# Second mixer: two decay projections of a head as seven block products instead of sixteen half-size ones, weight sums made by adding transfers

## The chip, the cores and the metric

The kernel runs on one core of a Trainium2 chip. The metric is device time in microseconds (us) for one execution of the whole program, median of several runs. The engines are TensorE (PE in the profile; its weight loads are PEld), VectorE (DVE), ScalarE (ACT), GpSimd (POOL) and SyncE (SP), which issues most of the transfers. All work in program order, each engine in its own queue; semaphores connect them.

## The reference, cut to what matters

Two layers of a diffusion backbone. The change is in the mixer of the second layer (`_odd_mixer`). `h` is the normed, modulated stream of 768 tokens (512 latent, then 256 context), 1024 wide; `w_in` is 1024 x 5120. Each of 8 heads has 128 query columns and 128 columns of decay logits for each direction:

```python
fq, f_fwd, f_bwd, fi, fog = _split(h @ w_in, ODD_SIZES)
q = _heads(jax.nn.silu(fq), HGRN_HEADS)
i = _heads(fi, HGRN_HEADS)
for d, f in enumerate((f_fwd, f_bwd)):
    log_f = jnp.logaddexp(jnp.log(lb[d]), jnp.log1p(-lb[d]) + jax.nn.log_sigmoid(_heads(f, HGRN_HEADS)))
    k = -jnp.expm1(log_f)
    dirs.append(_directional_scan(q, k, i, log_f, n_ctx, reverse=(d == 1)))
o_lat = _gated_readout(dirs[0][1] + dirs[1][1], og[:, :, n_ctx:], out_norm)
```

With s = sigmoid(f) the decay is `lb + (1-lb) s` and k is `(1-lb) - (1-lb) s`: two affine maps of the sigmoid with one scale and one bias per column. The context part is scanned first and gives the state `S0` from which the latent scan starts.

## The kernel before, in words

Every product of 32-bit operands is made of three matmuls on split operands: X = H + L, where H is X rounded by an ACT cast and L is the rest, by a DVE subtraction; the products are H·H, H·L and L·H (`mm3`). `h` lies on the chip split in this way for the whole mixer (tiles x: four of 128 x 3072). A weight is loaded as `raw` by SP, cast to `wH` by ACT (L803) and subtracted to `wL` by DVE (L804).

`odd_mixer` runs over 8 heads. For head hd a generator `prep` makes the decays of both directions and the query; a second generator, `head` (that is `scan`), does the chunked scan of the head's 512 latent tokens and its readout. In `prep` each direction d loads one unit of 1024 x 128 weights (512 KB) and does 48 matmuls of 128 x 256 (tokens 512 to 767) and 128 x 512 (tokens 0 to 511) each into the tile `ff`: 24 of either kind. ACT takes the sigmoid into `sg` (L1419) and one affine map of it each for the context and the latent tokens (L1424, L1426), DVE the other (L1423, L1425). Then 24 matmuls of 128 x 512 give `fq`, the query.

The order of the work is written out by hand: the loop calls `go(...)` with the steps of three heads in turn (query and decays of head hd, scan of head hd-1, readout of hd-2), and `pinned` keeps matmuls and transposes in that order. The other engines' instructions are placed around it by a scheduler at build time; once placed, an engine's queue is fixed. `raw` has three buffers of 512 KB, `wH` and `wL` four each, so a head's weights are fetched, cast and split well ahead of their matmuls.

In `scan`, DVE and ACT alternate over seven levels: ACT copies half of `arr` into `qkh` (L1012), DVE multiplies it by a decay (L1017) and squares up the decays (L1018). PE makes the score blocks (`pch`, `pbh`), transposes (`knph`, `kcT`), state updates (`pdh`) and the output (`poh`); ACT copies `pbh` to `STh` (L1049) and `knph` to `knh` (L1064), which `pdh` needs. In the readout POOL makes the reciprocal root (`rs`, L686).

The feed-forward of the first layer already multiplies by seven block products (`SEVEN`, `seven`), and its down projection already lets transfers from POOL add to what is on the chip (L1773).

Of the kernel before, what the change touches and what calls it, by code (L numbers as in the profile page):

```python
# [8 lines left out]
F32 = mybir.dt.float32  # L9
# [307 lines left out]
class Net:  # L317
# [24 lines left out]
    def banks(self, narrow):  # L342
        if self.ps is not None:
            self.ps.release()
        self.narrow = narrow
        self.ps = self.tc.alloc_tile_pool(name={True: "psn", False: "psw", None: "pso"}[narrow], bufs=1, space=PSUM, reuse_waits="tile")
# [21 lines left out]
    def sc_tile(self, name, which=None):  # L368
        if which is None:
            self.side = which = 1 - self.side  # L370
        return self.ps.tile([P, 512], F32, tag=f"sc{which}", bufs=1, name=name)

# [574 lines left out]
    def scan(self, pool, nm, arr, q, ksum, dscale, f, nt, hpp, V, first, ends, o_evac):  # L947
# [24 lines left out]
        CT = pool.tile([P, ns, 32], F32, tag="CT", bufs=1 if hpp > 1 else 2, name=f"CT{nm}")  # L972
# [29 lines left out]
        while b < P:  # L1002
            qk = pool.tile([P, 2, N], F32, tag=f"qk{N}", bufs=4 if N > CTX else 3, name=f"qk{nm}{b}")
# [64 lines left out]
        for d, (order, steps) in enumerate(orders):  # L1068
# [10 lines left out]
            for i, t in enumerate(steps):  # L1079
                S = pool.tile([P, P], F32, tag="S", bufs=8 if hpp > 1 else 10, name=f"S{nm}{d}{t}")  # L1080
# [318 lines left out]

    def odd_mixer(self, h, fi):  # L1400
        nc, I = self.nc, self.I
        w = I["odd_w_in"][0]
        with self.pool("hg") as gp:
            ones = gp.tile([P, CTX], F32, tag="ones", name="ones")
            nc.gpsimd.memset(ones, 1.0)
            def prep(hd, given):
# [3 lines left out]
                ks = gp.tile([P, SEQ], F32, tag="ks", bufs=2, name=f"ks{hd}")  # L1410
                S0, kcs = [], []
                for d in range(2):
                    pt = self.mm_tile(f"ff{hd}{d}")
                    W = self.unit_cols(w, (1 + d) * D + hd * P)
                    self.gemm_T(pt, W, h, ((512, 256),))
                    yield
                    self.gemm_T(pt, W, h, ((0, 512),))
                    sg = gp.tile([P, NT], F32, tag="sg", bufs=2, name="sg")
                    nc.scalar.activation(sg, pt[:, :NT], AF.Sigmoid)  # L1419
                    lb, lb1, nlb1 = (x[:, d, hd : hd + 1] for x in (self.lb, self.lb1, self.nlb1))  # L1420
                    fc = gp.tile([P, CTX + 32], F32, tag="fc", bufs=2, name="fc")
                    kc = gp.tile([P, CTX], F32, tag="kc", bufs=2, name="kc")
                    nc.vector.tensor_scalar(fc[:, :CTX], sg[:, SEQ:], lb1, lb, op0=ALU.mult, op1=ALU.add)  # L1423
                    nc.scalar.activation(kc, sg[:, SEQ:], AF.Identity, bias=lb1, scale=nlb1)  # L1424
                    nc.vector.tensor_scalar(f[:, d, :], sg[:, :SEQ], lb1, lb, op0=ALU.mult, op1=ALU.add)  # L1425
                    nc.scalar.activation(arr[:, 2 * d, :], sg[:, :SEQ], AF.Identity, bias=lb1, scale=nlb1)  # L1426

                    pr = gp.tile([P, CTX], F32, tag="pr", bufs=1, name="pr")
                    if d == 0:
                        nc.vector.memset(pr[:, CTX - 1 : CTX], 1.0)  # L1430
                        nc.vector.tensor_tensor_scan(
                            pr[:, 0 : CTX - 1][:, ::-1], fc[:, 1:CTX][:, ::-1], ones[:, 1:CTX], 1.0, op0=ALU.mult, op1=ALU.mult
                        )
                    else:
                        nc.vector.memset(pr[:, 0:1], 1.0)
                        nc.vector.tensor_tensor_scan(
                            pr[:, 1:CTX], fc[:, 0 : CTX - 1], ones[:, 1:CTX], 1.0, op0=ALU.mult, op1=ALU.mult
                        )
                    nc.vector.tensor_tensor(kc, kc, pr, op=ALU.mult)

                    kcs.append(kc)
                    yield
                pq = self.mm_tile(f"fq{hd}")
                self.gemm_T(pq, self.unit_cols(w, hd * P), h, ((0, 512),))
                q = gp.tile([P, SEQ], F32, tag="q", bufs=2, name=f"q{hd}")
                nc.scalar.activation(q, pq[:, :SEQ], AF.Sigmoid)
                nc.vector.tensor_tensor(q, q, pq[:, :SEQ], op=ALU.mult)
                nc.vector.tensor_tensor(arr[:, 1, :], q, f[:, 1, :], op=ALU.mult)
                nc.vector.tensor_tensor(arr[:, 3, :], q, f[:, 0, :], op=ALU.mult)
                nc.vector.tensor_tensor(ks, arr[:, 0, :], arr[:, 2, :], op=ALU.add)  # L1450
                given.append((arr, q, ks, f, S0))
                yield
                kns = []
                for kc in kcs:
                    pk = self.tr_tile("kcT")
                    for i in range(2):
                        self.tr(pk[:, i * P : (i + 1) * P], kc[:, i * P : (i + 1) * P], self.ident)
                    kn = gp.tile([P, CTX], F32, tag="kcn", bufs=2, name="kcn")
                    nc.scalar.copy(kn, pk[:, :CTX])
                    kns.append(kn)  # L1460
# [51 lines left out]
            def go(*xs):  # L1512
                for x in xs:
                    next(x, None)
# [770 lines left out]
```

## Time and profile before

| | |
|---|---|
| median of 3 runs | 1674.99 us (1674.77 to 1675.28) |
| the profiled execution's own time | 1675.78 us |
| its span, first to last instruction | 1674.0 us |
| mean granted clock of TensorE | 0.998 |
| PE busy | 1644.8 us, 98% of the span |
| DVE busy | 1311.1 us, 78% |
| ACT busy | 916.1 us, 55% |
| POOL busy | 129.4 us, 8% |
| the mixer's heads on PE | 982 to 1221 us of the span |

The profiled execution took 1.8 us more than its span, and lies 0.8 us above the median. Rows of a profile name the line, the engine, the operation, what is written and read (`out<-in`), the shape, the count, and then busy time and the mean duration of one in ns. A line of a helper stands for many calls: L355 is every matmul, so groups are told apart by the tile written (`ff`, `fq`, `poh`).

### The profile page before, as it was taken

How to read it: one execution, taken by the hardware profiler on the slowest of the kernel's cores; microseconds unless marked ns; L12 is line 12 of the kernel's file. 1: busy time of each engine (PE TensorE's matmuls, PEld its weight loads, DVE VectorE, ACT ScalarE, POOL GpSimd, SP SyncE). 2: the span in 40 equal slices, each digit the busy share in tenths (PEclk: the TensorE clock that was granted, in tenths of full speed). 3: DMA queues.
4: the chain of work that ended last, by engine and by line, in shares of the span. 5: the costliest groups of instructions: out<-in, count | busy, mean ns of one | idle time of the engine just before them, and what ended most of it. 6: DMA issues, size and time to landing. Idle time of an engine off the chain costs nothing.

```text
span 1674.0 us, 32524 instructions
## 1 busy us (share of the span) xinstructions
PE 1644.8 (98%) x13407; PEld 1481.1 (88%) x13407; DVE 1311.1 (78%) x2097; ACT 916.1 (55%) x1551; POOL 129.4 (8%) x139
## 2 busy tenths in 40 slices
PE   9999999999999999999999999999999999999998
PEld 7899987888999999998887888888888899999886
DVE  5999678976898988777668648788775599987887
ACT  5745567845544443446447436666664565555664
POOL 2004110011000000002102000000000100000310
PEclk9999999999999999999999999999999999999999
DMA  9641012164243445249525541121124333333973
GB/s 336 213 132 41 3 45 86 50 227 160 80 126 114 139 151 176 78 153 205 100 84 193 200 127 57 48 65 40 51 65 150 126 114 115 114 101 102 226 164 138
DMA packets 184736, 204.79 MB, mean 122 GB/s; under 512 B 7142, under 2 KB 141836, under 8 KB 184588
## 3 DMA queue, kind: packets, MB, share of 16 engines
q1 hardware_dynamic: 173996, 181.98, 34.7%
q0 software_dynamic: 9024, 17.30, 5.9%
q10 hardware_dynamic: 1568, 3.43, 0.6%
q8 instruction: 105, 1.72, 0.4%
q14 instruction: 43, 0.35, 0.1%
HBM read 193.23 MB, written 9.46 MB: 121 GB/s over the span
## 4 chain that ended last, share of the span: by engine, by line
PE 83%; DVE 8%; ACT 3%; DMA 3%; issue 2%; POOL 0%; SPq 0%; DVEq 0%; ACTq 0%; POOLq 0%
PE nat L355 12%; PE a L355 10%; PE ff L355 8%; PE E L355 7%; PE oproj L355 6%; PE x L355 6%; PE o L355 5%; PE D L355 4%; PE b L355 3%; PE fq L355 3%; PE gqk L355 2%; PE pearly L355 2%; PE q L355 2%; PE S L355 2%; PE poh L355 1%
## 5 line engine op out<-in xcount | busy, mean ns | idle before, releaser
L355 PE MATMUL nat<-wH,x 128*128 128x256 f32 (+2 forms) x968 | 226.7, 322 | 1.2 <-ACT x L2014 0.6
L860 ACT CAST wH<-raw 128x1024 fp32r<-128x1024 f32 x120 | 124.8, 1051 | 102.7 <-DVE raw L885 40.7
L355 PEld LDWEIGHTS nat<-wH,x 128*128 128x128 f32 x968 | 161.9, 190 | 19.5 <-ACT natq L1196 1.7
L861 DVE TENSOR_TENSOR wL<-raw,wH 128x1024 fp32r<-128x1024 f32 x120 | 145.7, 1222 | 23.6 <-ACT wH L860 23.3
L355 PE MATMUL nat<-wL,x 128*128 128x256 f32 (+2 forms) x484 | 153.5, 317 | 1.8 <-DVE wL L804 1.8
L804 DVE TENSOR_TENSOR wL<-raw,wH 128x1024 fp32r<-128x1024 f32 x79 | 95.8, 1222 | 50.6 <-ACT wH L803 49.8
L355 PE MATMUL ff<-x,wH 128*128 128x512 f32 (+1 forms) x512 | 127.6, 340 | 0.0
L686 POOL TENSOR_TENSOR rs<-ms,neghalf 128x1 f32<-128x1 f32 (+2 forms) x56 | 60.1, 1076 | 777.7 <-DVE ms L684 777.6
L803 ACT CAST wH<-raw 128x1024 fp32r<-128x1024 f32 x79 | 82.2, 1050 | 68.5 <-PE ff L355 19.7
L355 PE MATMUL oproj<-wH,x 128*128 128x512 f32 x320 | 102.2, 394 | 0.4 <-ACT x L1330 0.4
L355 PEld LDWEIGHTS nat<-wL,x 128*128 128x128 f32 x484 | 92.1, 190 | 7.8 <-DVE wL L804 2.7
L615 DVE SCALAR_TENSOR_TENSOR macc<-mraw,scT,macc 128x1024 f32<-128x1024 f32 x70 | 88.0, 1282 | 11.6 <-DMA mraw<-in_mod_w_dram 11.4
L355 PEld LDWEIGHTS ff<-x,wH 128*128 128x128 f32 x512 | 87.3, 190 | 10.0
L355 PE MATMUL x<-wH,two 128*128 128x512 f32 x280 | 90.5, 392 | 0.9 <-DVE y L1851 0.7
L1773 POOL DMA_DIRECT2D t<-in_ffn_w_down_dram x36 | 41.9, 1200 | 640.1 <-DVE t L1812 338.3
L1012 ACT COPY qkh<-arr 128x512 f32<-128x512 f32 x112 | 70.2, 641 | 36.6 <-DVE arr L1017 32.3
L355 PE MATMUL ff<-x,wL 128*128 128x256 f32 (+1 forms) x256 | 86.2, 337 | 0.0
L885 DVE TENSOR_TENSOR raw<-raw 128x512 f32<-128x512 f32 x120 | 82.8, 690 | 2.8
L1017 DVE TENSOR_TENSOR arr<-arr,f 128x512 f32<-128x512 f32 x112 | 74.4, 688 | 2.0 <-ACT qkh L1012 0.3
L355 PEld LDWEIGHTS oproj<-wH,x 128*128 128x128 f32 x320 | 59.9, 188 | 13.0 <-ACT x L1330 1.0
L355 PE MATMUL a<-T,wH 128*128 128x384 f32 (+1 forms) x320 | 70.5, 309 | 0.6 <-ACT qb L923 0.5
L355 PE MATMUL E<-T,wH 128*128 128x384 f32 (+1 forms) x320 | 70.4, 309 | 0.7 <-DVE go L938 0.7
(425 smaller groups left out, 4558.6 us busy)
## 6 DMA issues: line engine op xcount, KB each, us to landing
mraw<-in_mod_w_dram SPq DMA_DIRECT2D x80, 512.0 KB, 4.4
raw<-in_ffn_w_gate_dram SPq DMA_DIRECT2D x44, 512.0 KB, 3.9
raw<-in_ffn_w_up_dram SPq DMA_DIRECT2D x44, 512.0 KB, 4.9
raw<-in_odd_w_in_dram SPq DMA_DIRECT2D x40, 512.0 KB, 3.7
t<-in_ffn_w_down_dram POOLq DMA_DIRECT2D x30, 512.0 KB, 8.3
raw<-in_ffn_w_down_dram SPq DMA_DIRECT2D x28, 512.0 KB, 8.0
mraw<-in_mod_w_dram SPq DMA_DIRECT2D x32, 256.0 KB, 6.3
raw<-in_even_w_in_dram SPq DMA_DIRECT2D x16, 512.0 KB, 5.9
```

What stands on the lines that cost most here:

```text
L355: return self.pin(self.nc.tensor.matmul(*a, **k))
L615: nc.vector.scalar_tensor_tensor(a, u, w, a, op0=ALU.mult, op1=ALU.add)
L686: nc.gpsimd.tensor_tensor(rs, ms, self.neghalf.to_broadcast([P, w]), op=ALU.pow)
L803: self.casts = self.casts[-1:] + [nc.scalar.copy(H[:, :m], raw[:, :m])]
L804: vector.tensor_tensor(L[:, :m], raw[:, :m], H[:, :m].bitcast(F32), op=ALU.subtract)
L860: self.nc.scalar.copy(H, f)
L861: self.nc.vector.tensor_tensor(L, f, H.bitcast(F32), op=ALU.subtract)
L885: add = lambda o, x, y: nc.vector.tensor_tensor(o, x, y, op=ALU.add)
L1012: nc.scalar.copy(qkv[:, :, :, half, :], dst)
L1017: nc.vector.tensor_tensor(dst, dst, tb, op=ALU.mult)
L1773: add = lambda o, src: self.pin(nc.gpsimd.dma_start(out=o, in_=src, accum_op=ALU.add))
```

## The change

For heads 1 to 7 the two directions' projections become one product of a 256 x 1024 by a 1024 x 768 matrix, cut into two by two blocks on each side: the weight's blocks are `11`, `12` (forward columns, upper and lower 512 rows) and `21`, `22` (backward columns); `h`'s blocks are the first and second 512 rows by the first and second 384 tokens. Seven products of 512 x 128 by 512 x 384 (12 matmuls of 128 x 384 each) replace the eight that plain block multiplication needs. They use sums of weight blocks and of `h` blocks. Head 0 is done plainly, with eight products.

- `half_sums` makes the four sums of `h` blocks (T1 to T4) once, by DVE subtractions and additions of 128 x 1536 with splits, stepwise ahead of and between the products of head 0.
- The weight sums of a head: blocks are fetched by SP in six pieces of 256 KB; four transfers from POOL with `accum_op=ALU.add` then add further blocks from DRAM into tiles on the chip. `u2` gets two of them one after the other, `u1` and `w21` one each. A seventh operand is made by a DVE addition (`w12 + u2`).
- Seven operands and the query's two halves are each cast and split as 128 x 512, into a ring of four slots that lies in two of the four `wH`/`wL` buffers; the other two hold the scan's level copies (`levels`), which had buffers of their own (`qkh`).
- The four results are put together by ACT copies and four DVE operations on 128 x 384 (`c11`, `c12`, `c21`, `c22`, halves of two `sg` tiles); then the sigmoids. All four affine maps are ACT's now.
- The context's running product is written over `fc`; the readout's squares are written back to PSUM; a few tiles of the scan have fewer buffers. PSUM has single banks for this mixer (`banks(4)`), also under the gate product at the end, whose first weights go into the T tiles.

```diff
+    def half_sums(self, h, pool, temp):
...
+        def steps():
+            op(a, f32["22"][0], f32["12"][0], ALU.subtract)
+            op(b, f32["22"][1], f32["12"][1], ALU.subtract)
+            op(a, a, b, ALU.add)
+            split("T3", a)
...
+            op(a, a, f32["21"][1], ALU.subtract)
+            yield
+            split("T4", a)
...
+            ring = [[own[x][i // 2][:, 512 * (i % 2) : 512 * (i % 2) + 512] for x in "HL"] for i in range(4)]
+            levels = [own[x][i].rearrange("p (a n) -> p a n", a=2) for i in (2, 3) for x in "HL"]
...
+            order = [SEVEN[i] for i in (0, 4, 3, 1, 6, 2, 5)]
...
+            def raw():
+                r = self.wp.tile([P, WU], F32, tag="raw", bufs=3, name="raw")
+                return [r[:, 512 * i : 512 * i + 512] for i in range(2)]
+            def fetch(o, src):
+                nc.sync.dma_start(out=o.rearrange("p (k n) -> p k n", k=4), in_=src)
+            def add(o, src):
+                self.pin(nc.gpsimd.dma_start(out=o.rearrange("p (k n) -> p k n", k=4), in_=src, accum_op=ALU.add))
+            def operand(x):
+                H, L = turned(ring)
+                nc.scalar.copy(H, x)
+                nc.vector.tensor_tensor(L, x, H.bitcast(F32), op=ALU.subtract)
+                return [z.rearrange("p (k n) -> p k n", k=4) for z in (H, L)]
+            def weights(hd):
+                (w11, w12), (w21, w22) = x = raw(), raw()
...
+                u2, u1 = raw()
+                fetch(u2, block(0, 0, hd))
+                fetch(u1, block(1, 0, hd))
+                add(u2, block(1, 0, hd))
+                add(u1, block(1, 1, hd))
+                add(u2, block(1, 1, hd))
+                add(w21, block(0, 0, hd))
+                for x in (w11, w22, u2, u1, w21, w12):
+                    yield operand(x)
+                nc.vector.tensor_tensor(w12, w12, u2, op=ALU.add)
+                yield operand(w12)
...
-                for d in range(2):
-                    pt = self.mm_tile(f"ff{hd}{d}")
-                    W = self.unit_cols(w, (1 + d) * D + hd * P)
-                    self.gemm_T(pt, W, h, ((512, 256),))
-                    yield
-                    self.gemm_T(pt, W, h, ((0, 512),))
...
-                    nc.vector.tensor_scalar(f[:, d, :], sg[:, :SEQ], lb1, lb, op0=ALU.mult, op1=ALU.add)
+                    for wn, xn, b in order:
...
+                        product(pt, next(W), forms[xn], new, True)
+                        if wn == "11":
+                            nc.scalar.copy(c11, pt)
+                        elif wn == "22":
+                            nc.scalar.mul(c21, pt, -1.0)
+                            yield
...
+                            nc.vector.tensor_tensor(c12, c12, pt, op=ALU.add)
+                            sigmoid(c12)
+                            gates(0)
                     yield
...
-                self.gemm_T(pq, self.unit_cols(w, hd * P), h, ((0, 512),))
+                for k, x in enumerate(raw()):
+                    fetch(x, w[512 * k : 512 * k + 512, hd * P : hd * P + P].rearrange("(k p) m -> p k m", p=P))
+                    H, L = operand(x)
+                    product(pq, (H, L), [h.tiles[k][i][:, :, :SEQ] for i in range(2)], k == 0, k == 1)
...
-                go(scan, new)
-                go(outs, old)
-                go(new, new)
-                go(outs, old, scan)
-                go(new, new)
+                go(scan, old, new)
+                go(outs)
+                go(new)
+                go(old, outs, scan)
+                go(new, new, old)
                 go(scan, scan)
```

Where the instructions stand, at three places. POOL's queue in the mixer before: one `rs` for each head's readout.

```order
L686 TENSOR_TENSOR rs_11392<-ms_11390,neghalf_97 128x4
L686 TENSOR_TENSOR rs_11810<-ms_11808,neghalf_97 128x4
L686 TENSOR_TENSOR rs_12228<-ms_12226,neghalf_97 128x4
L686 TENSOR_TENSOR rs_12646<-ms_12644,neghalf_97 128x4
L686 TENSOR_TENSOR rs_13064<-ms_13062,neghalf_97 128x4
```

POOL's queue now, heads 5 and 6: `raw_12134` is the tile of u2 and u1 of head 5, `raw_12129` that of w21 and w22; `raw_12553` and `raw_12548` are head 6's. The three additions into a u tile are u2, u1, u2.

```order
L1485 DMA raw_12134<-in_odd_w_in_dram 128x4x128 x3
L1485 DMA raw_12129<-in_odd_w_in_dram 128x4x128
L689 TENSOR_TENSOR rs_12250<-ms_12248,neghalf_97 128x4
L1485 DMA raw_12553<-in_odd_w_in_dram 128x4x128 x3
L1485 DMA raw_12548<-in_odd_w_in_dram 128x4x128
L689 TENSOR_TENSOR rs_12669<-ms_12667,neghalf_97 128x4
```

Four transfers now stand in the queue ahead of each `rs`.

ACT's queue before, from the query of head 6 to the copies that head 5's state updates need:

```order
L803 CAST wH_13333<-raw_13331 128x1024
L1446 ACTIVATE q6_12818<-fq6_12787 128x512
L1049 COPY STh5_12859<-pbh5_12860 128x512
L1064 COPY knh50_12882<-knph50_12883 128x384
L1064 COPY knh51_12888<-knph51_12889 128x384
L1012 COPY qkh61_12895<-arr6_12496 128x512 x2
```

ACT's queue now at the same point, one head earlier in the numbers (scan of head 4, operands of head 6):

```order
L1641 COPY S040_12443<-S0_12438 128x128
L1641 COPY S041_12445<-S0_12438 128x128
L1490 CAST wH_10261<-raw_12553 128x512
L1015 COPY wL_10267<-arr5_12119 128x512
L1052 COPY STh4_12482<-pbh4_12483 128x512
L1067 COPY knh40_12505<-knph40_12506 128x384
L1067 COPY knh41_12511<-knph41_12512 128x384
L1015 COPY wL_10267<-arr5_12119 128x512
```

The cast of u2 (`raw_12553`), which needs both additions into u2, now stands ahead of `STh` and `knh`.

DVE's queue before, where the scan's levels of head 6 meet the weights and decays of head 7:

```order
L1018 TENSOR_TENSOR f6_12495<-f6_12495 128x2x32
L804 TENSOR_TENSOR wL_13340<-raw_13337,wH_13339 128x1024
L1423 TENSOR_SCALAR fc_13003<-sg_13001,lb1_782,lb_779 128x256
L1425 TENSOR_SCALAR f7_12913<-sg_13001,lb1_782,lb_779 128x512
L1431 SCALAR_TENSOR_TENSOR pr_13009<-fc_13003,ones_10253 128x255
```

DVE's queue now, at the end of head 6's decays (`raw_12818` is head 6's query weight, `ffE6` the bank that the last of the seven products ends in, `raw_12966` head 7's first weight):

```order
L1597 TENSOR_TENSOR sg_12540<-sg_12540,ffB6_12780 128x384
L1020 TENSOR_TENSOR arr5_12119<-arr5_12119,f5_12118 128x8x64 x2
L1600 TENSOR_TENSOR sg_12540<-sg_12540,ffE6_12626 128x384
L1021 TENSOR_TENSOR f5_12118<-f5_12118 128x2x4
L1491 TENSOR_TENSOR wL_10265<-raw_12818,wH_10261 128x512
L1491 TENSOR_TENSOR wL_10264<-raw_12966,wH_10260 128x512
```

The split of the query's second half stands behind the operation that needs the seventh product. The tile it frees is the one into which SP fetches the u2 and u1 of the next head.

210 lines of the change are left out of this document (158 added, 52 removed).

## The prediction

> **What bounds the kernel now.** I read the page first, then the busy time by stretch for one head of the second mixer, then the chain of waits over the same stretch.
>
> ```profile
> span 1674.0 us, 32524 instructions
> PE 1644.8 (98%) x13407; PEld 1481.1 (88%) x13407; DVE 1311.1 (78%) x2097; ACT 916.1 (55%) x1551; POOL 129.4 (8%) x139
> ```
>
> ```profile
> core 0: us, PE busy (x) PEld busy (x) DVE busy (x) ACT busy (x) POOL busy (x), PEclk, DMA share, GB/s
> 1063.44:1094.97 31.53, 31.53 (x401) 28.11 (x400) 25.14 (x57) 19.73 (x35) 1.44 (x1) 1.00 0.18 52
> ```
>
> ```profile
> 1018.22 5.68 PE ff L355 x24
> ...
> 1063.44 2.88 PE ff L355 x24
> 1066.32 1.34 PE pdh L355 x12
> 1067.66 0.44 PE kcT L358 x4
> 1068.10 8.35 PE ff L355 x48
> 1076.44 2.68 PE poh L355 x24
> 1079.13 0.89 PE S L355 x8
> 1080.02 1.25 PE pch L355 x83
> 1081.27 5.68 PE ff L355 x24
> 1086.95 5.44 PE fq L355 x24
> 1092.39 0.69 PE pch L355 x50
> 1093.08 1.08 PE pbh L355 x32
> 1094.17 0.80 PE knph L358 x6
> ```
>
> A head's period of 31.53 us is PE's own work without a gap; DVE has 6.4 us to spare in it and ACT 11.8. Saved PE work is saved time, as long as the other engines and the transfers keep up. That is the question here.
>
> **PE's side.** Twelve matmuls of 128 x 384 stand in the trace, in the first layer's seven products:
>
> ```profile
> 448.52 2.08 PE E L355 x12
> 982.29 16.68 PE ff L355 x96
> ```
>
> Seven products cost 7 x 2.08 = 14.56 us; the `ff` pieces above cost 2.88 + 8.35 + 5.68 = 16.91. PE's sum for a head falls by 2.35 to 29.18 us. Head 0, eight products, costs 16.64 against 16.68. Seven heads would give 16.5 us.
>
> **DVE and ACT.** Durations from one head:
>
> ```profile
> L1017 DVE TENSOR_TENSOR arr<-arr,f 128x512 f32<-128x512 f32 x14 | 9.3, 689 | 0.1
> L804 DVE TENSOR_TENSOR wL<-raw,wH 128x1024 fp32r<-128x1024 f32 x3 | 3.7, 1224 | 1.6 <-ACT wH L803 1.6
> L1425 DVE TENSOR_SCALAR f<-sg,lb,lb 128x512 f32<-128x512 f32 x2 | 1.1, 541 | 0.0
> L1439 DVE TENSOR_TENSOR kc<-kc,pr 128x256 f32<-128x256 f32 x2 | 0.8, 422 | 0.1
> L1489 DVE TENSOR_TENSOR fi<-fi,rs 128x512 f32<-128x512 f32 x1 | 0.7, 692 | 0.9 <-POOL rs L686 0.9
> L803 ACT CAST wH<-raw 128x1024 fp32r<-128x1024 f32 x3 | 3.1, 1048 | 3.0 <-PE fq L355 1.9 <-PE ff L355 1.1
> L1012 ACT COPY qkh<-arr 128x512 f32<-128x512 f32 x14 | 8.8, 643 | 4.9 <-DVE arr L1017 4.3 <-DVE arr L1448 0.4
> L1426 ACT ACTIVATE arr<-sg,lb,nlb 128x512 f32<-128x512 f32 x2 | 1.6, 807 | 3.4 <-PE poh L355 3.4
> L1064 ACT COPY knh<-knph 128x384 f32<-128x384 f32 x3 | 1.4, 489 | 0.0
> L1049 ACT COPY STh<-pbh 128x512 f32<-128x512 f32 x1 | 0.6, 587 | 0.5 <-PE pbh L355 0.5
> ```
>
> DVE loses three splits (3.67), the maps of f (1.08) and fc (about 2 x 0.41) and two memsets (0.1): 5.7. It gains nine splits of 128 x 512 (9 x 0.69 = 6.2), one weight addition (0.69) and four operations of 128 x 384, put between the 422 of 256 and the 689 of 512 columns at 0.55 each (2.2): 9.1. Successive instructions overlap by about 0.06, so for seven more of them 25.14 + 3.4 - 0.4 = 28.1 us. ACT loses three casts (3.1) and two sigmoids of 768 columns (taken as 0.8 each), 4.7; it gains nine casts (at 0.64: 5.8), four copies of 384 (2.0), sigmoids over the same columns in three pieces (1.8), two maps of 512 (1.6) and two of 256 (1.2): 12.4, so 27.4 us. Against PE's 29.18 nobody has room left; before, DVE's spare time was also spent waiting, 0.9 of it for `rs`. The removed level buffers, the PSUM square and the moved `go` steps I cost at nothing: the same count of instructions, behind PE's 29 us; that cover is thin, and the range has to pay for it.
>
> **The transfers.** u2 of the next head needs a fetch and two additions one after the other, and its tile is freed only by the split of the query's second half. The nearest rows are a fetch of 512 KB in the mixer, one of 256 KB in the feed-forward, and two lone additions of the down projection:
>
> ```profile
> raw<-in_odd_w_in_dram SPq DMA_DIRECT2D x40, 512.0 KB, 3.7
> raw<-in_ffn_w_down_dram SPq DMA_DIRECT2D x5, 256.0 KB, 2.6
> ```
>
> ```profile
> 802.68 0.91 POOL L1773 DMA_DIRECT2D t<-in_ffn_w_down_dram  x1 [23.77 <-DVE wL L1807]
> 806.94 1.22 POOL L1773 DMA_DIRECT2D t<-in_ffn_w_down_dram  x1 [3.35 <-DVE wL L1807]
> ```
>
> ```profile
> t<-in_ffn_w_down_dram POOLq DMA_DIRECT2D x1, 512.0 KB, 6.0
> t<-in_ffn_w_down_dram POOLq DMA_DIRECT2D x1, 256.0 KB, 4.2
> ```
>
> The fetch: between 2.6 and 3.7, taken as 2.8, since u1 is fetched beside it. An addition of 256 KB: there 128 runs of 2 KB, here 512 runs of 512 bytes. POOL's issue grows by 0.31 for 128 more runs, so by 0.9 for 384; if only the bytes count beyond that, it lands after 4.2 + 0.9 = 5.1; if every run costs what a further run of 2 KB does (6.0 - 4.2 = 1.8 for 128), after 4.2 + 3 x 1.8 = 9.6. I take 5.3: the 3.7 for 1024 short runs of a plain fetch shows bytes, not runs, as the limit there. Then C, from that split to u2 on the chip, is 2.8 + 2 x 5.3 + 0.2 for the hand-overs = 13.6 us; its ends are 2.6 + 2 x 4.2 = 11.0 and 3.7 + 2 x 9.6 = 22.9.
>
> A rule speaks against this price. The Trainium skill, "DMA: Bandwidth & Descriptors", in the section on the anatomy of one DMA on the SWDGE (gpsimd) path, fits 2.0 us plus the bytes at 436 GB/s: an estimate of 2.6 us for an addition of 256 KB, and so C = 2.8 + 5.2 + 0.2 = 8.2. The two rows above disagree with it, in the level and in the step from 256 to 512 KB (1.8 instead of 0.6).
>
> **What waits for it.** In ACT's new order the cast of u2 stands ahead of a level copy, `STh` and the two `knh`, and PE's `pdh` needs the last of these: 0.64 + 0.64 + 0.59 + 2 x 0.49 = 2.85, say 2.8 after u2 has landed. On the other side, DVE splits the query's second half only behind the addition of the seventh product's bank, so 0.55 + 0.17 + 0.69, about 1.3 us after PE has ended that product. From there to `pdh` PE has 5.44 + 0.89 + 0.69 + 1.08 + 0.80 + 2 x 2.08 = 13.06 us of work. So C is hidden up to 13.06 - 1.3 - 2.8 = 9.0; beyond that PE stands still, every head: 4.6 us at 13.6. The loop closes on itself (transfer, products, split, transfer), so nothing makes up for it later: the period is 29.18 + C - 9.0 = C + 20.2 on PE. DVE's part of the same loop is 28.1 less the 8 us that it does while the transfers run, plus a cast and the wait for `rs`: C + 21.6. What is queued behind the late u2 is thus ACT's copies for `pdh`, DVE's levels of the scan and, on POOL, the `rs` of the readout.
>
> **The clock.** PE's last matmul of the program ends at 1666.0:
>
> ```profile
> 1664.00:1666.00 2.00, 2.00 (x9) 1.31 (x7) 1.27 (x3) 0.84 (x2) 0.55 (x1) 1.00 0.66 266
> 1666.00:1668.00 2.00, 0.01 (x1) 0.00 (x0) 1.97 (x3) 0.26 (x1) 0.00 (x0) 1.00 0.07 27
> 1668.00:1670.00 2.00, 0.00 (x0) 0.00 (x0) 1.12 (x4) 0.46 (x2) 0.55 (x1) 0.68 0.58 236
> ```
>
> A mean of 0.68 over two microseconds, with 0.50 after, means that the clock was halved some 2.7 us into the idle time. A stall of 4.6 us would then be followed by matmuls at half speed; for how long, no row shows. If the clock needs as long to come back, 1.35 us are lost per head (bounds: nothing, and 4.2 if both products behind the stall run at half speed). PE's part is then C + 21.5, level with DVE's; I take C + 21.5.
>
> The Trainium skill, "TensorE: Matmul & The Clock Gate", part 1 on the HAM clock gate, has the clock halved after an idle window of about 3.4 us that runs freely, and restored after a busy window of that length; the rows above agree on the first. By it the loss would be 1.7 a head, and the sum 2.5 us higher.
>
> **Head 1 and the sums of h.** A DVE operation of 128 x 1536, by 689 and 1224 ns for 512 and 1024 columns, is 1.76 us; fourteen are 24.6. DVE is free for them from here:
>
> ```profile
> 975.01 0.69 DVE L487 COPY modrows<-mod_acc 128x512 f32<-128x512 f32 x1 [2.25 <-PE mod_acc L355]
> ```
>
> Thirteen of them (1.70 each with overlap), four splits (2.5) and small work (0.7) stand ahead of the split of head 0's second query half: 975.7 + 25.3 = 1001 us. PE has head 0 to do until 982.29 + 16.64 + 5.44 = 1004.4 and two products of head 1 until 1008.6; u2 is split at 1001 + C + 1.4 = 1016.0. From there PE needs 4.16 + 0.44 + 1.25 + 6.24 + 5.44 = 17.5 to the end of the query, 1033.5, with the clock's 1.35 about 1035; before it ended at 1018.22 + 5.68 + 5.44 = 1029.3. Head 1 costs C - 8.
>
> **The sum.** Six periods (heads 2 to 7) of C + 21.5 - 31.53, and head 1: 6 x (C - 10.0) + C - 8 = 7C - 68; at C = 13.6 it is +27 us. The profiled execution of 1675.8 would become 1703, and the median, 0.8 below it, 1702. C at which the gain and the loss meet is 9.7 by this sum, 11 if the clock holds and PE alone closes the loop (7C - 77). The gate product behind the heads has weights in slots freed by then, and the first feed-forward is untouched: nothing for both.
>
> **Rivals.**
> - The additions land in time (C below 9.5). Against it: 4.2 us, twice, and a fetch, all measured. For it: the lone rows are few, and PE's own sum surely falls. Period 29.4, DVE's 28.1 with waits: 7 x -2.1, less 1 us while head 1 waits for T4 (DVE's last sum): 1661 us. By the rule of the page on DMA quoted above, this is the case. Chance 0.13.
> - The loop and the saving cancel (C of 10 to 11, clock held): 1672 to 1678 us. 0.07.
> - Each short run costs like a long one: C of 17 and up, 7C - 68 from +51: 1726 to 1767 us. For it: an addition reads what it writes. Against it: plain fetches of short runs are quick. 0.13.
> - The forecast, C from 11 to 17: 1684 to 1726. 0.67.
>
> That the seven products are not done is excluded: PE's queue has 12 matmuls of 384 columns fewer per head. Faster by over 0.2%, within 0.2% and slower by over 0.2% (about what a measurement of this kernel can tell from no change) are 0.13, 0.07 and 0.80. The range of 1676 to 1738 leaves out the first rival, part of the second, and the upper part of the third.
>
> **What would show it.** Right: PE idle in each of heads 2 to 7 ahead of `pdh` or the third product, released by ACT's `knh` or DVE's split, with the addition on POOL behind it; periods near 35 us; additions landing after 5 to 6 us; the granted clock below 1 in these stretches; PE busy lower by some 16 us apart from the clock. Wrong: additions that land in under 4 us, or periods near 29.5 with PE unbroken; or a period set by DVE's or ACT's own work, without a wait for a transfer.

## The result, and the profile after

The changed kernel takes 1770.5 us (median of four runs, 1769.0 to 1771.7) against 1674.9: ratio 1.057, interval 1.0552 to 1.0588. It is slower, as forecast, but by 95.6 us where 27 were predicted, beyond the range of 1676 to 1738.

The first lines of the profile after, with the busy time of each engine:

```profile
span 1768.6 us, 32677 instructions
PE 1662.1 (94%) x13323; PEld 1506.0 (85%) x13323; DVE 1349.8 (76%) x2143; ACT 959.6 (54%) x1669; POOL 163.9 (9%) x166
```

PE has 84 matmuls fewer (seven heads by twelve) and yet more busy time, at a lower clock. The busy time by stretch, for one head from one `knph` to the next, before:

```profile
core 0: us, PE busy (x) PEld busy (x) DVE busy (x) ACT busy (x) POOL busy (x), PEclk, DMA share, GB/s
1094.10:1125.62 31.52, 31.52 (x402) 28.09 (x398) 25.12 (x57) 19.69 (x34) 1.43 (x1) 1.00 0.18 52
```

and after:

```profile
1133.19:1177.59 44.40, 34.21 (x391) 31.58 (x387) 27.62 (x62) 24.93 (x49) 6.27 (x5) 0.88 0.37 73
```

A head takes 44.40 us and no engine fills it: DVE's 27.6 is near the 28.1 estimated, ACT's 24.9 is 2.5 below its 27.4, and PE idles for 10 us, with a mean granted clock of 0.88 over the head. The timeline of POOL in one head shows what the time goes into. A row gives the start, the duration, and in brackets how long the engine was idle before it and what ended that:

```profile
1130.23 1.33 POOL L1485 DMA_DIRECT2D raw<-in_odd_w_in_dram  x1 [10.45 <-DVE qks L1604]
1136.70 1.31 POOL L1485 DMA_DIRECT2D raw<-in_odd_w_in_dram  x1 [5.13 <-DMA raw<-in_odd_w_in_dram]
1141.70 1.29 POOL L1485 DMA_DIRECT2D raw<-in_odd_w_in_dram  x1 [3.70 <-issue]
1146.83 1.30 POOL L1485 DMA_DIRECT2D raw<-in_odd_w_in_dram  x1 [3.83 <-issue]
```

These are the additions to u2, u1, u2 and V (`w21`), issued 6.5, 5.0 and 5.1 us apart. The first gap ends when a transfer has landed. The other two have no releaser that the profile shows ("issue"), and V's addition waits in the program for nothing of the other three. The lines of ACT, DVE and SP's DMA queue (SPq) in the same stretch follow them:

```profile
1126.70 0.37 SPq L1482 DMA_DIRECT2D raw<-in_odd_w_in_dram  x1
...
1141.47 0.62 ACT L1490 CAST wH<-raw 128x512 fp32r<-128x512 f32 x1 [9.41 <-DMA raw<-in_odd_w_in_dram]
...
1146.54 0.62 ACT L1490 CAST wH<-raw 128x512 fp32r<-128x512 f32 x1 [1.56 <-DMA raw<-in_odd_w_in_dram]
...
1151.72 1.14 ACT L1490 CAST wH<-raw 128x512 fp32r<-128x512 f32 x2 [3.61 <-DMA raw<-in_odd_w_in_dram]
...
1152.38 0.69 DVE L1491 TENSOR_TENSOR wL<-raw,wH 128x512 fp32r<-128x512 f32 x1 [3.29 <-ACT wH L1490]
...
1153.09 0.37 SPq L1482 DMA_DIRECT2D raw<-in_odd_w_in_dram  x1
...
1156.29 0.62 ACT L1490 CAST wH<-raw 128x512 fp32r<-128x512 f32 x1 [0.39 <-DMA raw<-in_odd_w_in_dram]
...
1157.18 0.65 ACT L1626 COPY kc<-kcT 128x256 f32<-128x256 f32 x2
```

Read in order: the query's split frees the tile and u2 is fetched (1126.70); u1 has landed at 1141.47, u2 at 1146.54, V at 1151.72. V's split (1152.38) frees the query's tile, so the query's weights are fetched only at 1153.09, cast at 1156.29, and behind that cast ACT's queue holds the copies of the context's transposes (1157.18), on which PE waits for `poh`. From the fetch of u2 to the cast of V are 25 us of the 44.4.

### The profile page after: what moved, and what is told of

Same layout as the page of the kernel before. It is cut to its first block, busy times and chain, and to the rows that moved or that the text cites. A ratio compares the mean times of both kernels' runs of the same rounds, so it can differ in the third digit from the quotient of the medians.

```text
span 1768.6 us, 32677 instructions
## 1 busy us (share of the span) xinstructions
PE 1662.1 (94%) x13323; PEld 1506.0 (85%) x13323; DVE 1349.8 (76%) x2143; ACT 959.6 (54%) x1669; POOL 163.9 (9%) x166
## 3 DMA queue, kind: packets, MB, share of 16 engines
q1 hardware_dynamic: 181772, 185.65, 33.7%
## 4 chain that ended last, share of the span: by engine, by line
PE 70%; issue 11%; DVE 8%; ACT 5%; DMA 4%; POOL 2%; SPq 0%; DVEq 0%; POOLq 0%; ACTq 0%
PE nat L355 11%; PE a L355 11%; PE E L355 7%; PE oproj L355 6%; PE x L355 6%; PE o L355 4%; PE D L355 4%; PE b L355 4%; PE gqk L355 2%; PE pearly L355 2%; DMA raw<-in_odd_w_in_dram 2%; PE q L355 2%; POOL raw L1485 1%; PE attO L355 1%; PE S L355 1%
## 5 line engine op out<-in xcount | busy, mean ns | idle before, releaser
L355 PE MATMUL nat<-wH,x 128*128 128x256 f32 (+2 forms) x904 | 206.2, 317 | 1.2 <-ACT x L2183 0.6
L863 ACT CAST wH<-raw 128x1024 fp32r<-128x1024 f32 x120 | 124.8, 1050 | 103.6 <-DVE raw L888 41.1
L355 PEld LDWEIGHTS nat<-wH,x 128*128 128x128 f32 x904 | 149.9, 190 | 17.1 <-ACT natq L1199 1.7
L864 DVE TENSOR_TENSOR wL<-raw,wH 128x1024 fp32r<-128x1024 f32 x120 | 145.8, 1222 | 22.9 <-ACT wH L863 22.5
L355 PE MATMUL nat<-wL,x 128*128 128x256 f32 (+2 forms) x452 | 141.0, 312 | 1.9 <-DVE wL L807 1.9
L1490 ACT CAST wH<-raw 128x512 fp32r<-128x512 f32 x69 | 41.7, 617 | 118.6 <-DMA raw<-in_odd_w_in_dram 100.3
L1942 POOL DMA_DIRECT2D t<-in_ffn_w_down_dram x36 | 41.9, 1197 | 639.7 <-DVE t L1981 338.6
L1491 DVE TENSOR_TENSOR wL<-raw,wH 128x512 fp32r<-128x512 f32 x69 | 46.4, 689 | 44.6 <-ACT wH L1490 44.4
L807 DVE TENSOR_TENSOR wL<-raw,wH 128x1024 fp32r<-128x1024 f32 x51 | 61.5, 1221 | 20.1 <-ACT wH L806 19.4
L355 PEld LDWEIGHTS oproj<-wH,x 128*128 128x128 f32 x320 | 60.0, 188 | 13.6 <-ACT x L1333 1.6
L355 PE MATMUL E<-x,wH 128*128 128x384 f32 (+1 forms) x320 | 70.6, 310 | 0.0
L355 PE MATMUL b<-x,wH 128*128 128x384 f32 (+1 forms) x320 | 70.5, 309 | 0.0
L355 PE MATMUL a<-x,dH 128*128 128x384 f32 (+1 forms) x320 | 70.3, 309 | 0.0
```

Source lines behind the costliest of these rows:

```text
L355: return self.pin(self.nc.tensor.matmul(*a, **k))
L807: vector.tensor_tensor(L[:, :m], raw[:, :m], H[:, :m].bitcast(F32), op=ALU.subtract)
L863: self.nc.scalar.copy(H, f)
L864: self.nc.vector.tensor_tensor(L, f, H.bitcast(F32), op=ALU.subtract)
L1490: nc.scalar.copy(H, x)
L1491: nc.vector.tensor_tensor(L, x, H.bitcast(F32), op=ALU.subtract)
```

## The experiments

**1. No additions at all** (u2, u1 and V keep one plain block; the sums are left out).

```
-                add(u2, block(1, 0, hd))
-                add(u1, block(1, 1, hd))
-                add(u2, block(1, 1, hd))
-                add(w21, block(0, 0, hd))
```

> The four additions of heads 1 to 7 are left out (u2, u1 and V then hold one plain block each, so the decays are not those of the reference); fetches, products, order and buffers stay. Theory S (POOL carries one addition of 512 short runs at a time, about 5.05 us each and 6.5 for the first of a head; with the fetch 25 us of the 44.4 us period): the loop from the query's split to u2 shrinks to the fetch of 3.5 us, PE runs through, periods of 29.5 to 31, time 1658 to 1672. Rival E (the new order of ACT's and DVE's work is itself too long for a head, and the additions only hide that): periods of 33 and more, time above 1685.

Measured: 1684.6 us (before, beside it, 1674.2; ratio 1.0061, 1.0045 to 1.0076). So the additions cost 86 of the 96 us. The other 10 fit neither theory's numbers: the time lies just under rival E's 1685, and a head takes 32.24 us, between the two.

```profile
1097.33:1129.57 32.24, 30.02 (x391) 28.03 (x387) 27.36 (x62) 25.04 (x50) 1.01 (x1) 1.00 0.23 67
```

PE is busy for 30.0 of it (29.18 was estimated) and the clock is whole.

**2. V's addition first on POOL.**

```
+                add(w21, block(0, 0, hd))
                 fetch(u2, block(0, 0, hd))
...
-                add(w21, block(0, 0, hd))
```

> Only the place of V's addition changes: first of the four on POOL instead of last. Its tile is free some 10 us before the query's split, so under theory S it leaves the chain behind that split: u1, u2 land as before, V no longer 5.1 us after them; seven heads give up to 7 x 5.1 = 36 us back, time 1733 to 1745. Rival Q (what counts is POOL's queue as a whole, four additions a head, wherever they stand): unchanged, 1765 to 1775.

Measured: 1744.6 us (1.0419, 1.0405 to 1.0433), 26 us less than the change: theory S's direction, at the upper end of its range. POOL's queue has the same work as before, so its sum is not the bound; the place of an addition in the chain is.

**3. Each addition as two of 256 runs.**

```
+                for k in (0, 2):
+                    y = o[:, 128 * k : 128 * k + 256].rearrange("p (k n) -> p k n", k=2)
+                    self.pin(nc.gpsimd.dma_start(out=y, in_=src[:, k : k + 2], accum_op=ALU.add))
```

> Each addition is issued as two of 256 runs of 512 bytes. Theory R (the queue behind POOL holds so many runs that one addition of 512 fills it, and the next waits until the first has landed): two or three halves are under way at once, u2 lands 4 to 8 us earlier in each head, time 1710 to 1745. Rival O (POOL waits for each addition to land before it issues the next, whatever its size): a half costs 2.0 + 1.2 + 0.6 = 3.8 us, eight of them 30 against 20 us, time 1820 to 1850.

Measured: 1721.1 us (1.0284, 1.0270 to 1.0298), 49 us less, with the same bytes and runs in twice as many instructions. POOL's timeline for a head:

```profile
1146.21 3.75 POOL L1487 DMA_DIRECT2D raw<-in_odd_w_in_dram  x3 [10.56 <-ACT wH L1492]
1150.83 6.20 POOL L1487 DMA_DIRECT2D raw<-in_odd_w_in_dram  x5 [0.86 <-issue]
```

Three halves are issued back to back in 3.75 us, then five more in 6.2; all eight take 11 us from the first issue to the last, where the four whole ones took 18 (1130.23 to 1148.13). The landing times (the last number) from the lists of DMA issues, of the changed kernel

```profile
raw<-in_odd_w_in_dram POOLq DMA_DIRECT2D x28, 256.0 KB, 4.7
```

and of this one:

```profile
raw<-in_odd_w_in_dram POOLq DMA_DIRECT2D x56, 128.0 KB, 3.9
```

Rival O (each waits for the one ahead, whatever its size) is refuted. Theory R fits: 768 runs were issued without a pause, 512 and 512 never. That the limit is the room in the queue behind POOL is inferred from this; the queue itself is in no view. The Trainium skill, "DMA: Bandwidth & Descriptors", section SWDGE vs HWDGE vs iDMA, says that POOL writes such a transfer's descriptors into rings in SBUF which the DMA engines drain; it gives no number of runs at which POOL has to wait.

**4. The sums on DVE**, from blocks that are on the chip.

```
+                nc.vector.tensor_tensor(u1, w21, w22, op=ALU.add)
+                nc.vector.tensor_tensor(u2, w11, u1, op=ALU.add)
+                nc.vector.tensor_tensor(w21, w21, w11, op=ALU.add)
```

> u1 = w21 + w22, u2 = w11 + u1 and V = w21 + w11 are formed on DVE from the blocks that are on the chip already; no additions on POOL, two fetches fewer per head. Theory S: three operations of 128 x 512 are 2.07 us, DVE's sum for a head 27.6 + 2.0 = 29.6, level with PE's 29.2; periods of 30 to 31.2, time 1662 to 1675. Rival E (DVE's and ACT's order is too long): periods over 32, time above 1680.

Measured: 1687.3 us (1.0078, 1.0065 to 1.0090), as rival E said. The head takes 32.24 us again, to the digit, with 1.8 us more work on DVE:

```profile
1100.02:1132.26 32.24, 30.02 (x391) 28.03 (x387) 29.14 (x65) 24.93 (x49) 1.01 (x1) 1.00 0.18 51
```

So DVE's sum does not set the 32.24. PE's waits in this head, from the list of waits (us in total, times, the longest):

```profile
PE pbh L355 <- ACT S L1638: 1.0, 1, 1.0
...
PE poh L355 <- ACT kc L1623: 0.8, 1, 0.8
...
PE fq L355 <- DVE sg L1594: 0.5, 1, 0.5
```

**5 and 6. The sums on POOL's arithmetic, and the maps of f and fc back on DVE.** The edit of 4 with `nc.gpsimd` for `nc.vector`; in 6 also

```
-                    nc.scalar.activation(f[:, d, :], x, AF.Identity, bias=lb, scale=lb1)
+                    nc.vector.tensor_scalar(f[:, d, :], x, lb1, lb, op0=ALU.mult, op1=ALU.add)
```

and the same for fc.

> The three sums u1 = w21 + w22, u2 = w11 + u1, V = w21 + w11 are formed by POOL's own arithmetic on blocks that are on the chip; no additions by transfers. Theory S with C (the transfers cost all but some 10 us of the loss; what is left is a closed loop of small steps through ACT, 32.2 us a head, which no engine fills): as the kernel without sums, 1683 to 1690, if POOL needs under 3 us for an operation. Rival D (with the sums on DVE it was DVE's 29 us of work that set the 32.2): DVE is back at 27.4, periods fall below 31.5, time under 1678.

> As the kernel with the sums on POOL, and the maps of f and fc back on DVE as before the change (four operations fewer on ACT, 2.8 us; four more on DVE, about 1.9 us). Theory A (the loop of 32.2 us a head is closed by ACT's queue, sigmoids and maps ahead of the copies that PE waits for): 1 to 2 us a head back, time 1670 to 1679. Rival D (DVE is the bound of the loop): 1 to 2 us a head more, 1690 to 1702.

Measured: 1694.5 us (1.0118, 1.0103 to 1.0133) and 1703.5 us (1.0178, 1.0161 to 1.0195). Both theories missed the first; theory A missed the second clearly, rival D by 1.5 us. DVE is busy for 29.4 us in a head of 5, with the same 62 instructions that took 27.4 in experiment 1, and for 32.0 in one of 6:

```profile
1069.08:1102.13 33.05, 30.09 (x391) 28.04 (x387) 29.41 (x62) 24.92 (x49) 5.81 (x4) 1.00 0.17 50
...
1106.96:1141.06 34.10, 30.30 (x391) 28.09 (x387) 31.98 (x66) 22.55 (x45) 4.94 (x4) 1.00 0.17 48
```

In 6 that is 2.7 more than 27.4 and the 1.9 of the maps: POOL's arithmetic slows DVE (last section). So 5 did not give DVE its 27.4 back, and 6 does not tell A from D cleanly.

**7 and 8. u2 and u1 in the slot that is free earlier**, with whole additions and with halves.

```
+                if hd:
+                    u2, u1 = raw()
+                    fetch(u2, block(0, 0, hd))
+                    fetch(u1, block(1, 0, hd))
                 (w11, w12), (w21, w22) = x = raw(), raw()
...
-                u2, u1 = raw()
-                fetch(u2, block(0, 0, hd))
-                fetch(u1, block(1, 0, hd))
```

> Additions by transfers as in the change; only the tile of u2 and u1 is taken and fetched ahead of the other two tiles of its head, so that it takes the slot that the last product's split frees, some 9.4 us before the query's second split. Theory S (a loop of slot, fetch and four additions in series): the period falls by about 9 us to 35, time 1700 to 1715. Rival Q (the additions on POOL are the bound by themselves): unchanged, 1765 to 1775.

> As the kernel before it, with each addition issued as two of 256 runs. By theory S with R (several halves under way at once) u2 is ready before PE asks for it, and what is left is the loop without sums: 1683 to 1692. If the two gains lie on the same wait they do not add, and it ends where one of them alone did, 1700 to 1720.

Measured: 1716.8 us (1.0255, 1.0239 to 1.0270) and 1699.6 us (1.0148, 1.0126 to 1.0171). An earlier slot with the same additions gives 54 us back: the loop over the slot is shown, rival Q refuted. The period fell to about 38, less than the forecast of 35, and with halves to between 34.0 and 36.8: the gains add in part, and 15 us more than without additions remain.

**9 to 12. Pieces of work moved off DVE and ACT**, on the kernel with sums on DVE, and one part of the change on the kernel before it:

```
-                    nc.vector.tensor_tensor(o, o, rs[:, :, None].to_broadcast([P, LT, P]), op=ALU.mult)
+                    nc.gpsimd.tensor_tensor(o, o, rs[:, :, None].to_broadcast([P, LT, P]), op=ALU.mult)
...
-                    nc.scalar.activation(kcs[d], x, AF.Identity, bias=lb1, scale=nlb1)
+                    nc.gpsimd.tensor_scalar(kcs[d], x, nlb1, lb1, op0=ALU.mult, op1=ALU.add)
```

and, on the kernel before the change,

```
-                    nc.vector.tensor_scalar(f[:, d, :], sg[:, :SEQ], lb1, lb, op0=ALU.mult, op1=ALU.add)
+                    nc.scalar.activation(f[:, d, :], sg[:, :SEQ], AF.Identity, bias=lb, scale=lb1)
```

with the same for fc (in 10 and 11 for fc as well as kc, in 12 for fc as well as f).

> Sums on DVE as in the earlier kernel (period 32.24), and the scaling of a finished head by its rs moved from DVE to POOL, right behind the rs that POOL computes: DVE loses 0.69 of work and 0.9 of waiting per head. Theory L (a loop through PE, ACT, DVE and POOL closes each head: finished head, ss, rs, scaling, levels, sums of the gates, sigmoids and maps, copies of S, next head): the scaling's round trip is in it, 1 to 1.6 us a head back, period 30.6 to 31.3, time 1676 to 1681. Rival P (the two waits of PE for ACT alone, with ACT's maps ahead of the copies, close the loop): unchanged, 1685 to 1689.

> Sums on DVE, and the four context maps of 128 x 256 moved from ACT to POOL (2.3 us of ACT's work a head, 1.08 of it between the query and the copies of S that PE waits for). Theory P: the wait of 1.0 us at pbh goes, period 31.2, time 1678 to 1682. Theory L alone: the loop is shorter by the same 1.0 at most and by nothing if DVE's scan of the context then comes late: 1680 to 1690.

> Both moves together. If they are two pieces of one loop (theory L) their gains add: 2 to 2.6 us a head, PE close to unbroken at 29.6 to 30.3, time 1668 to 1675. If either one alone opens the loop and another closes it, no better than the better of the two.

> The kernel before the change with one part of it: the maps of f and fc on ACT instead of DVE, both projections as they were. ACT has 11.8 us to spare in a head there and DVE loses 1.9 us. Both theories: PE's 31.53 us a head stay unbroken, 1672 to 1677; if ACT's longer queue delays the copies that PE waits for even there, 0.5 to 1 us a head more, 1678 to 1682.

Measured: 1686.5, 1687.8 and 1685.7 us (1.0069, 1.0085, 1.0070, each within 0.0016), all within 2 us of the kernel of 4. Theory L missed 9 and 11, theory P missed 10 (9 is unchanged, as it said), so neither is borne out, with the reservation that POOL's work again slowed DVE: a head of 11 has 29.6 us of DVE's work, with less to do than the 29.1 of experiment 4. The maps alone, on the kernel before: 1674.6 us (1.0002, 0.9992 to 1.0011). That part of the change costs nothing where ACT has room.

**13 and 14. Two of PE's waits taken away**: the query in another PSUM bank, the context transposes ahead of U1's product; with the sums on DVE, and with the sums left out.

```
-                pq = self.acc_tile(2, f"fq{hd}")
+                pq = self.acc_tile(banks["D"], f"fq{hd}")
...
-                go(new)
-                go(old, outs, scan)
+                go(new, old, new)
+                go(outs, scan)
```

> Sums on DVE; the query's product written to the bank of the 22 product (free early) instead of that of the 12 product, and the context transposes ahead of the U1 product instead of behind it. Of PE's 2.2 us of waits a head these take away the two for the bank (0.45) and for the copies of the transposes (0.79). Theory W (PE's own waits are the 32.24 - 30.0; each that goes is time): period 31.0, time 1677 to 1680. Theory D (DVE, 29.1 us of work and 3 us of short waits, closes the loop of 32.2 by itself): PE's wait moves elsewhere, period 31.9 to 32.3, time 1685 to 1689.

> The same two moves with the sums left out altogether (decays not those of the reference): DVE has 27.4 us of work instead of 29.1. Theory D: the period falls by what DVE has less, to 30.2 to 31.2, time 1668 to 1677. Theory W: as the kernel with sums on DVE and the same moves, within 2 us.

Measured: 1682.7 us (1.0051, 1.0037 to 1.0065) and 1680.0 us (1.0035, 1.0022 to 1.0049). A head with the sums

```profile
1097.66:1128.86 31.20, 29.55 (x391) 28.07 (x387) 29.24 (x65) 24.95 (x49) 1.01 (x1) 1.00 0.18 52
```

and without them:

```profile
1095.08:1126.30 31.22, 29.57 (x390) 28.10 (x386) 27.43 (x62) 25.05 (x50) 1.01 (x1) 1.00 0.24 69
```

One microsecond a head less in both, whether DVE has 29.2 or 27.4 us of work: the period goes theory W's way, against D. The time fell by 4.6 us only in either case: 13 misses W's 1677 to 1680, and 14 lies 2.7 us below 13, where W allowed 2. The stretch that starts at the last head's `knph` takes 33.6 us in both, instead of 32.0, and head 1's first product now waits for head 0's query, 2.0 us without the sums and 2.5 with them:

```profile
PE ffA L355 <- DVE qks L1610: 2.5, 1, 2.5
```

**15. Two additions instead of four**, against the kernel of 13: u1's first block is fetched again, V's addition goes first, then u1's; u2 is made by one operation on DVE.

```
+                fetch(u1, block(1, 0, hd))
+                add(w21, block(0, 0, hd))
+                add(u1, block(1, 1, hd))
...
+                nc.vector.tensor_tensor(u2, w11, u1, op=ALU.add)
```

> The same two moves; V and u1 by one addition each on POOL (V's first, it is free early), u2 = w11 + u1 by one operation on DVE, so nothing is added twice in series: DVE 27.8 us a head, POOL's two additions 5 us each, the second landing some 10 us after the query's second split (3.5 + 6.5), about when PE asks for U2. Theory D with S: period 30.5 to 31.5, time 1670 to 1680. If u1 is late even so, 1 to 3 us a head more, 1680 to 1695.

Measured: 1725.2 us (1.0302, 1.0288 to 1.0316). Worse than any forecast. One fetch and one addition behind the query's split are already late. In a middle head ACT has to wait 3.2 us until u1 has landed (its cast starts at 1116.27), DVE forms u2 only at 1121.97, behind levels of the scan, and PE waits for u2's cast:

```profile
PE ffA L355 <- ACT wH L1490: 3.6, 1, 3.6
```

**16 and 17. The order moved further** (S ahead of the query, head 0's query in a bank of its own), against the kernel of 13, with the sums on DVE, and with V's sum by a transfer.

```
-                go(new, new, old)
+                go(new, old, new)
...
-                pq = self.acc_tile(banks["D"], f"fq{hd}")
+                pq = self.acc_tile(banks["D" if hd else "A"], f"fq{hd}")
```

In 17 also V's sum by an addition, and u1 from a block that is fetched for it:

```
-                nc.vector.tensor_tensor(u1, w21, w22, op=ALU.add)
+                fetch(u1, block(1, 0, hd))
+                add(w21, block(0, 0, hd))
+                nc.vector.tensor_tensor(u1, u1, w22, op=ALU.add)
...
-                nc.vector.tensor_tensor(w21, w21, w11, op=ALU.add)
```

> As the kernel with sums on DVE, the bank and the transposes moved, and two more moves of order: the context's state product S ahead of the query (so that ACT copies S before the maps that are late), and the first head's query in a bank that head 1 doesn't ask for at once. Theory W: PE's last wait of 1.7 a head at pbh goes, and 2.5 us in head 1: period 29.5 to 30.2, time 1668 to 1675. Theory D: DVE's 29.3 us with 1.6 of waits a period (30.9) is met first: 31.0, time 1676 to 1681.

> As the kernel beside it, and one of the three sums, V, by one addition on POOL, first in its head and far from being asked for; u1 = fetched w21 + w22 and u2 = w11 + u1 stay on DVE, 0.65 us less a head there. Theory W: as its neighbour within 2 us. Theory D: 0.5 us a head less than its neighbour, some 3 us faster. If the late fetch of u1 (3.5 us behind the query's split) shows as a wait of PE: 5 to 10 us slower.

Measured: 1680.7 us (1.0037, 1.0025 to 1.0049) and 1687.7 us (1.0083, 1.0071 to 1.0096). The time of 16 is theory D's, not W's, so neither theory holds for 13, 14 and 16 together. The wait at `pbh` is gone, but another has taken its place: the next head's first product waits for DVE's query product, and DVE has only short waits left.

```profile
PE ffA L355 <- DVE qks L1610: 1.4, 1, 1.4
...
DVE fi L1654 <- POOL rs L689: 0.9, 1, 0.9
DVE wL L1491 <- ACT wH L1490: 0.7, 1, 0.7
DVE fc L1553 <- ACT fc L1546: 0.3, 1, 0.3
DVE ss L1652 <- ACT poh L1650: 0.3, 1, 0.3
```

17 is 7 us slower than 16, within the 5 to 10 forecast for a late fetch of u1, but its trace doesn't show that fetch as the cause: heads of 30.2 and 30.7 us stand between heads of 34 to 35, with PE waiting for DVE's splits and query product. Which step makes the long ones stays open.

**18. Less on DVE**: the scaling by rs on ACT, the query in the bank that V leaves, the same order for the last head.

```
+                    for t in range(LT):
+                        nc.scalar.activation(o[:, t, :], o[:, t, :], AF.Copy, scale=rs[:, t : t + 1])
```

> As the kernel with the order moved, and 1.6 us a head taken off DVE: the scaling of a finished head by rs (0.69 of work and 0.9 of waiting for POOL) goes to ACT as four operations of 128 x 128; also the query's product in the bank that V leaves, where the next head's first product doesn't wait for it (1.4 us of PE's waiting), and the two moves of order for the last head, too. Theory D (DVE's 29.2 us with 2.2 of waits set the 31.4 us of the kernel with the order moved): the period falls to 29.7 to 30.5, time 1668 to 1676. If ACT's queue, with the wait for rs now in it, takes over as the bound: 31.2 to 32.5, time 1677 to 1688.

Measured: 1683.4 us (1.0055, 1.0041 to 1.0068), a head of 31.29 us:

```profile
1126.96:1158.25 31.29, 30.00 (x390) 27.93 (x387) 28.85 (x64) 25.81 (x55) 1.01 (x1) 1.00 0.18 52
```

Theory D's gain in a head did not come: heads take 31.1 to 31.9 us, in 16 31.4 to 31.8. The number fits the other forecast, but that ACT is the bound is not shown by it: 18 is 2.7 us above 16 because the last stretch takes 37.3 us instead of 33.7, with PE waiting up to 3.7 us for DVE's split of the gate product's first weights. What closes the last 1.3 us between PE's 30.0 and the 31.3 of a head stays open. No version beat the kernel before; the best with the sums done is that of 16, 1.0037 of its time.

## Why the prediction was right and wrong

**Right: the mechanism.** Slot, fetch and additions form a closed loop that outlasts PE's work; experiments 1, 2, 7 and 8 show it. Over all heads PE's largest repeated waits (us in total, times, the longest) are at `pdh` and at the third product (`ffA`), as forecast, and at `poh`, which was not:

```profile
PE pdh L355 <- ACT knh L1067: 23.7, 5, 5.3
PE poh L355 <- ACT kc L1626: 18.2, 6, 4.8
PE ffA L355 <- ACT sg L1582: 10.7, 6, 5.3
```

DVE's sum (28.1 estimated, 27.6 measured) holds; ACT's came out lower (24.9 for 27.4).

**Wrong: the term C**, "2.8 + 2 x 5.3 + 0.2 = 13.6". The price of an addition was near (5.3 taken; 4.7 to land, 5.0 to 5.1 from issue to issue). Only its issue was over-priced: 1.3 us for 512 runs, where 0.91 and three times 0.31 make 1.8. What failed is the number of additions in series. The prediction counted u2's two and let u1's, which stands between them in POOL's queue, run beside them; the trace has them one after the other. C, from 1126.70 to the cast at 1146.54, is 19.8: a fetch of 3.5, 6.5 for the first addition, 5.0 and 4.8. The prediction's own sum, 7C - 68, gives +71 with that C. So it is not the third rival, which put the same times down to short runs that cost like long ones.

**Left out: the fourth addition.** V's stood behind the three, and no term priced it. Its split frees the query's tile, and the query's late cast holds up ACT's copies for `poh`. The period is 44.4 where C + 21.5 gives 41.3. Experiment 2 takes V out of the series: of its heads 1 to 6, one takes 38.8 us and the others 40.6 to 41.9, as in the stretch below, and the kernel gets 26 us back. That is about the step from +71 to +96.

```profile
1162.42:1203.07 40.65, 32.79 (x390) 30.15 (x386) 27.53 (x62) 24.81 (x49) 6.26 (x5) 0.92 0.40 79
```

**Wrong in a detail: which cast stands first.** `STh` and `knh` stand behind u1's cast, not u2's: ACT's cast at 1141.47 follows the second addition, u1's, and starts before the second one into u2 is issued (1141.70). The tile that the section on the change names for this cast holds both u2 and u1. PE's wait at `pdh` so ended with u1, and u2 came 5 us later:

```profile
1143.54 2.93 PE L355 MATMUL pdh<-fi,knh 128*128 128x128 f32 x12 [5.31 <-ACT knh L1067]
```

That these 5.3 us look like the 4.6 forecast is luck: u1 was cast 14.8 us after the fetch, close to the 13.6 taken for u2, but the two additions in series up to there are u2's first and u1's own, not the two into u2.

**The clock's term** was too small and beside the point. The stretches after the wait at `pdh`:

```profile
1143.00:1147.00 4.00, 2.93 (x12) 2.63 (x12) 3.12 (x8) 2.44 (x6) 0.17 (x1) 0.50 0.54 66
1147.00:1152.50 5.50, 4.91 (x15) 4.91 (x16) 2.02 (x4) 1.89 (x5) 1.13 (x1) 0.50 0.39 48
1152.50:1157.00 4.50, 2.28 (x14) 2.01 (x13) 4.50 (x12) 4.11 (x9) 0.00 (x0) 0.99 0.40 117
```

Half speed lasted 9 us, and `pdh` with U2's product and part of U1's lost about 4 us, the upper bound (4.2), not 1.35. But PE then waited 2.8 us at `poh` for ACT in the same head, and what released it there hung on V's transfer, not on PE; so the loss was hidden in a wait that was there anyway.

```profile
PE poh L355 <- ACT kc L1626: 2.8, 1, 2.8
```

**The first rival's number (1661) was wrong too.** With the additions gone the kernel takes 1684.6: "saved PE work is saved time" needs an order in which PE never waits, and the new one has PE wait 2.2 us a head (32.24 less 30.02) for small steps of ACT and DVE (experiment 4), on a PE sum of 30.0 instead of 29.2. That is more than the 2.35 us a head that the products were to save. The rule of the Trainium skill that spoke for this rival ("DMA: Bandwidth & Descriptors", the anatomy of one DMA on the SWDGE path; by its fit an addition of 256 KB is estimated at 2.6 us) is not borne out: the additions landed after 4.7 us, and the measurement decides.

## What to carry to other kernels

Count every transfer that shares an issuing queue with the one you wait for, not only those that depend on it, and look how many can be under way at once: halving the transfers gave back 49 us without a byte less. A buffer slot that is freed late by the consumer starts the whole chain late, and giving the chain another slot was worth 54 us. On a kernel whose main engine has no gap, work taken off that engine is a gain only if nothing new makes it wait. Here the transfers did, and without them small steps of ACT and DVE did.

## What the runs showed of the hardware

- Additions of 512 runs of 512 bytes left POOL one at a time, some 5 us apart, while three of 256 runs were issued within 3.75 us.
- DVE is slowed by POOL's arithmetic. In experiment 11 POOL scaled a 128 x 512 tile at 1118.98 for 1.09 us, and two DVE operations beside it took 2.13 us (the timeline of 11):

```profile
1118.98 1.09 POOL L1652 TENSOR_TENSOR fi<-fi,rs 128x512 f32<-128x512 f32 x1
...
1118.49 2.13 DVE L1020 TENSOR_TENSOR arr<-arr,f 128x512 f32<-128x512 f32 x2
```

  The same pair in experiment 4 took 1.29:

```profile
1120.54 1.29 DVE L1020 TENSOR_TENSOR arr<-arr,f 128x512 f32<-128x512 f32 x2
```

- The granted clock was halved about 4.1 us into a wait of PE (1138.2 to 1142.4) and came back about 9 us after its next matmul (1143.54 to 1152.6), with PE busy for most of them; in the rows of the prediction it was halved after 2.7 us. So the traces give no fixed length of idle time, and the agreement that the prediction reads in its rows is only a rough one.

```profile
1142.00:1142.50 0.50, 0.00 (x0) 0.00 (x0) 0.00 (x0) 0.50 (x2) 0.50 (x1) 0.87 0.00 0
...
1152.50:1152.75 0.25, 0.25 (x2) 0.25 (x2) 0.25 (x1) 0.25 (x1) 0.00 (x0) 0.78 0.00 0
```
